# The low halves of the recurrent unit's input weights, made and stored during the first feed-forward

## The chip, the cores and the metric

The kernel runs on one core of a Trainium2 chip. TensorE (PE) multiplies, VectorE (DVE), ScalarE (ACT) and GpSimd (POOL) work on tiles in on-chip memory, SyncE (SP) and POOL issue most DMA transfers. The metric is the device time of one launch in microseconds, lower is better; before the change it is 1498.38 us, the median of three runs (1497.87 to 1498.54).

## What is computed

One step of a two-layer backbone on 640 tokens (512 latent, 128 context) of width 1024, all in fp32. Layer 0 mixes tokens with attention, layer 1 with a gated linear recurrence in both directions, and each is followed by a SwiGLU feed-forward of width 2816. The reference, shortened (in the kernel's names `w_in` is `wi`, `w_gu` is `gu`, `w_down` is `dn`, the recurrence's `w_out` is `wlo`, `w_mod` is `wm`):

```python
def _modulate(x, g, shift, scale):                      # adaLN of an RMS norm
    return _rms_norm(x, g) * (1 + scale[:, None, :]) + shift[:, None, :]

def _swiglu(x, w_gu, w_down):
    gate, up = jnp.split(x @ w_gu, 2, axis=-1)
    return (jax.nn.silu(gate) * up) @ w_down

def _lru_mixer(xm, h0, w_in, conv_w, conv_b, w_a, b_a, w_i, b_i, lam, w_out):
    gate, xr = jnp.split(xm @ w_in, 2, axis=-1)
    xc = _centred_depthwise_conv(xr, conv_w, conv_b)
    a_f, b_f = _rglru_coeffs(xc, w_a[0], b_a[0], w_i[0], b_i[0], lam[0])
    a_b, b_b = _rglru_coeffs(xc, w_a[1], b_a[1], w_i[1], b_i[1], lam[1])
    hs_f, hT_f = _linear_scan(a_f, b_f, h0[:, 0], reverse=False)
    hs_b, hT_b = _linear_scan(a_b, b_b, h0[:, 1], reverse=True)
    y = (hs_f + hs_b) * jax.nn.gelu(gate)
    return y @ w_out, jnp.stack([hT_f, hT_b], axis=1)

for i in range(2):                                      # layer 0 attention, layer 1 recurrence
    sh1, sc1, g1, sh2, sc2, g2 = silu(cond) @ w_mod[i] + b_mod[i]
    x = x + g1 * mixer_i(_modulate(x, norm_g[i, 0], sh1, sc1))
    x = x + g2 * _swiglu(_modulate(x, norm_g[i, 1], sh2, sc2), w_gu[i], w_down[i])
y = _rms_norm(x, final_g)
```

## The kernel before

Activations lie transposed, features on the 128 partitions and tokens along a row, as eight tiles of 128 x 640. A weight matrix is cut into tiles of 1024 x 128 (128x1024 on the chip, 512 KB). PE multiplies in a rounded fp32 form, so every operand is split in two: a high part, the value rounded, and a low part, the value minus the high part. A product is the sum of three matmuls for each of eight steps k: high by high (L239), high weight by low activation (L240), low weight by high activation (L241). These three lines are nearly all of PE's work.

`unit` (L170) makes one split weight tile. SP reads it into `raw`, of which there are three buffers for the whole kernel (L165); the high part `whi` is a cast on ACT (L186) or, in a phase whose only shared PSUM tag is `at`, a second transfer on POOL's queue that casts as it lands (L184); the low part `wlo` is a subtraction on DVE (L188). Where a phase has a second set of weight buffers, the same parts are called `whx` and `wlx`. `ws` and `project` then run the tile over the token chunks and hand each filled PSUM bank to an evacuation on DVE or ACT.

The phases follow one another: `start`, `attn`, `ffn0`, `lru`, `ffn1`. `ffn0` first adds the attention's output projection `wo` to `x` (`project`, DVE L639 for the residual, L623 for the low part of the scaled result, L578 for the sum of squares `ssq`), then forms the norm's statistics (`stats`): PE sums squares over partitions (L592, L595), DVE makes `var` (L597), POOL `rs` (L599), DVE the diagonal `dg` (L601), PE spreads it over partitions (`rr`, L609), ACT copies it to `r` (L633). This is done twice, for the second and the first half of the tokens, and `dg` and `rr` have one buffer each. Since the gate and up products do not need `r` (the norm's factor is applied when they are evacuated, DVE L1007, L1015, L1018), PE can run ahead of the statistics, up to five PSUM banks far (three `mm`, two `mx`). The feed-forward runs in three parts of 8, 7 and 7 hidden tiles (`ci` in `ffn`); each has gate and up products (`ws`), then the down projection (`project`; in the last part `project_closing`, which also forms the norm ahead of the recurrent layer: `nv` L614, high part L615 on ACT, low part L616 on DVE).

Beside this runs a generator, `modulations`: `w_mod` comes in 80 tiles of 512 KB over POOL's queue (L264, `mraw`, two buffers), and DVE forms two products with each (L268, `mprod`, one buffer). A call `fill(n)` takes n steps of it, one tile a step; `FG` and the phase's `quota` say how many. What is due sooner is pulled by `need`.

In `lru` the 16 tiles of `wi` are used through `halves` (L1366): eight for `xr`, which goes on to the convolution and the gates (`gp`, L1407), eight for the GeLU gate. `highs` (L1093) are the first matmuls of the output projection that follows.

The order of the instructions on each engine is not written by hand: a scheduler with a model of times sets it when the kernel is built. `pin` and `issue_after` put one instruction behind another in that order. Each engine then runs its list strictly in order.

Of the kernel before, what the change touches and what calls it, by code (L numbers as in the profile page):

```python
# [9 lines left out]
F32 = mybir.dt.float32  # L10
F32R = mybir.dt.float32r
AF = mybir.ActivationFunctionType
ALU = mybir.AluOpType
AX = mybir.AxisListType

P = 128
D = 1024
# [18 lines left out]
NLT = 10  # L36
C0 = 515
LATPR = (slice(0, 512), slice(C0, LW))
FG = (1, 1, 1)
MODS = ((0, 2), (0, 4), (0, 3), (0, 5), (1, 1), (1, 0), (1, 4), (1, 3), (1, 2), (1, 5))  # L40
NB = 2
KH = KT // 2
# [85 lines left out]
class _Step:  # L128
# [38 lines left out]
        self.read = self.nc.sync.dma_start(t, src).ins  # L167
        return t

    def unit(self, src, slot=None, after=None, nx=3, cast=False, raw=None):  # L170
        nc = self.nc
        _, a, b = src.shape
        raw = self.raw(src) if raw is None else raw
        if slot is None:
            self.nu += 1
            slot = "x" if self.wx and self.nu % 2 == 0 else "m"
        if slot == "x":
            hi, lo = self.wxs([P, a, b], nx)
        else:
            hi = self.t([P, a, b], F32R, "whi", 3)  # L180
            lo = self.t([P, a, b], F32R, "wlo", 3)
        if cast or self.ptags == ["at"]:
            with self.pin(self.cast if after else None):
                nc.gpsimd.dma_start(hi, src)  # L184
        else:
            nc.scalar.copy(hi, raw)  # L186
        with self.pin(after):
            self.low = nc.vector.tensor_tensor(lo, raw, hi.bitcast(F32), ALU.subtract).ins  # L188
        return hi, lo
# [70 lines left out]
    def mod_cols(self, l, j, out):  # L260
        nc = self.nc
        for f in range(KT):
            w = self.t([P, D], F32, "mraw", 2, self.sb)
            nc.gpsimd.dma_start(w, self.i["wm"][l * 6 + j - 2, f])  # L264
            for s in range(2):
                prod = self.t([P, D], F32, "mprod", 1, self.sb)
                with self.tc.issue_after(self.anchor) if self.anchor else nullcontext():
                    nc.vector.scalar_tensor_tensor(prod, w, 1.0, self.csb[:, s], ALU.mult, ALU.mult, accum_out=out[:, s, f:f + 1])  # L268
            yield
        nc.vector.tensor_tensor(out, out, self.col(f"bm{l}{j}").unsqueeze(1).broadcast_to([P, 2, KT]), ALU.add)  # L270
# [15 lines left out]
    def modulations(self):  # L286
        yield from self.mod_gate(0, 2)
        yield from self.mod_ss(0, 3, 1)
        yield from self.mod_gate(0, 5)
        yield from self.mod_ss(1, 0, 0)  # L290
        yield from self.mod_ss(1, 3, 1)
        yield from self.mod_gate(1, 2)
        yield from self.mod_gate(1, 5)

    def fill(self, n):
        for _ in range(min(n, self.quota)):
# [697 lines left out]
    def ffn(self, l, hi, lo, fp, last):  # L994
        nc = self.nc
        f0 = 0
        for ci, n in enumerate((8, 7, 7)):
            hhi = self.big()
            hlo = self.big()
            sg = {}  # L1000

            def eg(j):
                def ev(t0, s, ps):
                    if t0:
                        sg[j] = self.t([P, NTOK], F32, "sg", 2, fp)
                    g = sg[j]
                    nc.vector.tensor_tensor(g[:, s], ps, self.rt[:, s], ALU.mult)  # L1007
                    for c, a, b in _pieces(s.start, s.stop):
                        nc.scalar.activation(g[:, a:b], g[:, a:b], AF.Silu, bias=self.bias[:, c:c + 1])
                return ev  # L1010

            def eu(j):
                def ev(t0, s, ps):
                    u = self.t([P, 320], F32, "up", 2, fp)
                    nc.vector.tensor_tensor(u, ps, self.rt[:, s], ALU.mult)  # L1015
                    for c, a, b in _pieces(s.start, s.stop):
                        g = sg[j][:, a:b]
                        nc.vector.scalar_tensor_tensor(g, u[:, a - t0:b - t0], self.bias[:, c:c + 1], g, ALU.add, ALU.mult)  # L1018
                    self.split(hhi[:, j, s], hlo[:, j, s], sg[j][:, s])
                return ev  # L1020
            for j in range(n):
                f = f0 + j
                self.ws(self.i["gu"][l, f], hi, lo, eg(j), FG[0] * (f > 0), CHB)
                self.ws(self.i["gu"][l, NF + f], hi, lo, eu(j), FG[1] * (f > 0), CHB)
            w = self.i["dn"][l, :, :, f0:f0 + n]
            if ci == 2:
                last(w, hhi, hlo, (l, 5))
            else:
                self.project(w, hhi, hlo, (l, 5), done=lambda f: self.fill(FG[2]))
            f0 += n  # L1030


# [330 lines left out]
        c = CI["ba0"] * KT  # L1363
        nc.vector.tensor_scalar(self.hb, self.cols[:, c:c + 4 * KT], 0.5, None, ALU.mult)

    def halves(self, w, hi, lo, ev, after=None, slot=None):  # L1366
        u = self.unit(w, slot, after, 2)
        return [lambda t0=t0, t1=t1, **kw: ev(t0, self.chunk(u, hi, lo, t0, t1, **kw)) for t0, t1 in CHL]

    def lru_xr(self, f, hi, lo, after=None):  # L1370
        xr = self.xrs[f % 2]
        nat = xr[:, 2:514].rearrange("p (r c) -> p c r", r=ROWS)

        def ev(t0, ps):
            for o, a, b, r in ((nat[:, 56:64], 0, 64, ROWS), (nat[:, 0:40], 64, 384, ROWS),
                               (nat[:, 40:56], 384, 512, ROWS), (xr[:, 517:645], 512, 640, 0)):
                if t0 <= a and b <= t0 + 384:
                    v = ps[:, a - t0:b - t0]
                    self.nc.scalar.copy(o, v.rearrange("p (c r) -> p c r", r=r) if r else v)
        return self.halves(self.i["wi"][KT + f], hi, lo, ev, after)  # L1380

    def turn(self, table, step):
        if table != self.table:
# [126 lines left out]
    def lru_gate(self, f, hi, lo, lp, after=None):  # L1510
# [3 lines left out]
        def ev(t0, ps):  # L1514
# [3 lines left out]
                return  # L1518
            for v, o in ((G, G),) if f == KT - 1 else ((ps, G[:, t0:NTOK]), (G[:, 0:t0], G[:, 0:t0])):
                self.turn(AF.Gelu_apprx_tanh, lambda: nc.scalar.activation(o, v, AF.Gelu_apprx_tanh))  # L1520
        return G, self.halves(self.i["wi"][f], hi, lo, ev, after)

    def new_x(self, st):
        pool = st.enter_context(self.tc.tile_pool(name="x", bufs=1, reuse_waits="tile"))
# [6 lines left out]
    def run(self):  # L1531
# [11 lines left out]
        nc.vector.memset(self.ones, 1.0)  # L1543
        self.st = self.t([P, 2 * KT], F32, "st", 1)
        self.cs = self.t([P, 2 * KT], F32, "cs", 1)
        dram = self.ctx.enter_context(tc.tile_pool(name="dram", bufs=1, space=bass.MemoryType.DRAM))
        mpool, xpool = ExitStack(), ExitStack()
        self.csb = self.t([P, 2, D], F32, "csb", 1, mpool.enter_context(tc.tile_pool(name="mods", bufs=1)))
        self.mask = self.t([P, 64], F32, "mask", 1)
# [11 lines left out]
        V = self.big(F32, PITCH)  # L1561
        V = V.rearrange("p k t -> p (k t)")[:, 0:NT * D].rearrange("p (t d) -> p t d", t=NT)
        O = self.big(F32)
        with self.phase("attn", tp=2, sp=2, op=1, quota=24) as ap:
            self.kz = [self.t([P, 2, 960], F32R, f"KZ{j}", 1, ap) for j in range(2)]

# [29 lines left out]
        self.new_x(xpool)  # L1596
        self.load_x(i["x"])
        xd = dram.tile([D, NTOK], F32, tag="xd", name="xd")
        with self.phase("ffn0", at=2, rr=1, mx=2, wx=2, quota=56) as fp:
            self.project(i["wo"], ohi, olo, (0, 2), ((0, 1), xhi, xlo), None, True)  # L1600

            def last(w, hhi, hlo, gk):
                self.nh, self.nl = self.big(n=PITCH), self.big(n=PITCH)
                self.project_closing(w, hhi, hlo, gk, (1, 0), self.nh, self.nl, xd)
            self.ffn(0, xhi, xlo, fp, last)
        xpool.close()
        mpool.close()
        xhi, xlo = self.nh, self.nl
# [73 lines left out]
```

## Time and profile before

| | before |
|---|---|
| median of three runs | 1498.38 us |
| profiled execution | 1496.74 us |
| its span | 1494.9 us |
| instructions | 26171 |
| ACT busy | 698.6 us (47%) |
| POOL busy | 225.7 us (15%) |
| DMA traffic | 198.88 MB, mean 133 GB/s |

The profile is one execution. Busy times are those of each engine's own instructions; a line such as L188 is a line of the kernel before. `x16` is a count, and in square brackets stands the idle time before an instruction with what ended it. The profiled execution lies 1.64 us below the median of the three runs, and 1.84 us of it lie outside the span.

### The profile page before, as it was taken

The numbers are of one execution on the slowest core, as the hardware profiler recorded it, in microseconds if no ns is written. First come the engines' busy times: TensorE is split into PE (matmuls) and PEld (weight loads), VectorE is DVE, ScalarE is ACT, GpSimd is POOL, SyncE is SP. The second block draws the span as 40 slices with busy tenths as digits, with TensorE's granted clock in tenths as the row PEclk, the third lists the DMA queues.
The fourth block names the chain that finished last, engine by engine and source line by source line (L and its number), as shares of the span: only waits on it lengthen the run. The fifth ranks groups of instructions, "written<-read, shape, count | busy, mean of one in ns | idle before, by whom it ended". The sixth has DMA issues, their size and how long they took to land. (4 is left out here: it accounts for less than half of the span.)

```text
span 1494.9 us, 26171 instructions
## 1 busy us (share of the span) xinstructions
PE 1475.9 (99%) x10399; PEld 1433.0 (96%) x10399; DVE 1062.0 (71%) x2019; ACT 698.6 (47%) x1269; POOL 225.7 (15%) x264
## 2 busy tenths in 40 slices
PE   9999999999999999999999999999999999999997
PEld 7999999899999999999999988899999999999997
DVE  5778998679999987444443769886975666655645
ACT  5676667754332123312321569875634343424243
POOL 0212132101111110000000100000331322232311
PEclk9999999999999999999999999999999999999999
DMA  9645665345566664222222444335333131313111
GB/s 378 201 128 177 196 189 163 105 156 183 196 187 195 207 197 142 63 85 85 66 62 96 142 145 126 115 115 194 102 130 98 57 114 57 113 57 111 59 57 71
DMA packets 73050, 198.88 MB, mean 133 GB/s; under 512 B 8128, under 2 KB 24672, under 8 KB 72800
## 3 DMA queue, kind: packets, MB, share of 16 engines
q1 hardware_dynamic: 57360, 142.31, 29.9%
q0 software_dynamic: 14960, 54.21, 11.8%
q8 instruction: 82, 1.34, 0.4%
q10 hardware_dynamic: 608, 0.69, 0.1%
q14 instruction: 40, 0.33, 0.1%
HBM read 181.05 MB, written 8.92 MB: 127 GB/s over the span
## 5 line engine op out<-in xcount | busy, mean ns | idle before, releaser
L240 PE MATMUL mm<-big,whi 128*128 128x320 f32 (+3 forms) x1193 | 371.2, 311 | 0.8 <-DVE big L1508 0.6
L239 PE MATMUL mm<-big,whi 128*128 128x320 f32 (+3 forms) x1193 | 369.0, 311 | 1.6 <-ACT big L615 0.6
L241 PE MATMUL mm<-big,wlo 128*128 128x320 f32 (+3 forms) x1193 | 368.8, 310 | 0.0
L239 PEld LDWEIGHTS mm<-big,whi 128*128 128x128 f32 x1193 | 223.9, 188 | 3.7 <-ACT big L615 0.9
L240 PEld LDWEIGHTS mm<-big,whi 128*128 128x128 f32 x1193 | 224.2, 188 | 2.8 <-DVE big L1508 1.0
L241 PEld LDWEIGHTS mm<-big,wlo 128*128 128x128 f32 x1193 | 224.7, 188 | 1.1
L268 DVE SCALAR_TENSOR_TENSOR mprod<-mraw,csb 128x1024 f32<-128x1024 f32 x160 | 194.8, 1218 | 11.3 <-DMA mraw<-in_wm 10.8
L639 DVE SCALAR_TENSOR_TENSOR x<-mm,G,x 128x128 f32<-128x128 f32 (+3 forms) x193 | 77.4, 433 | 78.5 <-PE mm L241 77.0
L186 ACT CAST whi<-raw 128x1024 fp32r<-128x1024 f32 (+1 forms) x70 | 72.8, 1040 | 106.1 <-PE mm L240 71.2
L188 DVE TENSOR_TENSOR wlo<-raw,whi 128x1024 fp32r<-128x1024 f32 (+1 forms) x87 | 105.1, 1208 | 23.9 <-ACT whi L186 11.0
L240 PE MATMUL mm<-big,whx 128*128 128x320 f32 (+3 forms) x363 | 112.2, 309 | 0.0
L241 PE MATMUL mm<-big,wlx 128*128 128x320 f32 (+3 forms) x363 | 112.1, 309 | 0.0
L239 PE MATMUL mm<-big,whx 128*128 128x320 f32 (+3 forms) x363 | 111.9, 308 | 0.0
L264 POOL DMA_DIRECT2D mraw<-in_wm x80 | 43.4, 543 | 355.5 <-DVE mprod L268 257.3
L240 PE MATMUL mx<-big,whi 128*128 128x320 f32 (+3 forms) x299 | 92.1, 308 | 0.0
L239 PE MATMUL mx<-big,whi 128*128 128x320 f32 (+3 forms) x299 | 91.9, 307 | 0.0
L241 PE MATMUL mx<-big,wlo 128*128 128x320 f32 (+3 forms) x299 | 91.8, 307 | 0.0
L186 ACT CAST whx<-raw 128x1024 fp32r<-128x1024 f32 (+1 forms) x38 | 39.1, 1028 | 94.1 <-PE mm L240 54.5
L1506 ACT CAST whi<-raw 128x1024 fp32r<-128x1024 f32 (+1 forms) x41 | 41.3, 1007 | 69.0 <-PE mm L240 43.0
L240 PE MATMUL mx<-big,whx 128*128 128x320 f32 (+3 forms) x234 | 72.9, 312 | 0.0
L241 PE MATMUL mx<-big,wlx 128*128 128x320 f32 (+3 forms) x234 | 72.6, 310 | 0.0
L239 PE MATMUL mx<-big,whx 128*128 128x320 f32 (+3 forms) x234 | 72.4, 309 | 0.0
(409 smaller groups left out, 3734.3 us busy)
## 6 DMA issues: line engine op xcount, KB each, us to landing
raw<-in_gu SPq DMA_DIRECT2D x88, 512.0 KB, 3.5
mraw<-in_wm POOLq DMA_DIRECT2D x80, 512.0 KB, 3.9
raw<-in_dn SPq DMA_DIRECT2D x24, 512.0 KB, 3.6
sw<-in_wm SPq DMA_DIRECT2D x16, 512.0 KB, 10.2
raw<-in_wqk SPq DMA_DIRECT2D x16, 512.0 KB, 4.9
raw<-in_wi SPq DMA_DIRECT2D x16, 512.0 KB, 3.5
whi<-in_wi POOLq DMA_DIRECT2D x16, 512.0 KB, 3.8
raw<-in_dn SPq DMA_DIRECT2D x16, 448.0 KB, 3.3
```

The source lines that it names most:

```text
L186: nc.scalar.copy(hi, raw)
L188: self.low = nc.vector.tensor_tensor(lo, raw, hi.bitcast(F32), ALU.subtract).ins
L239: nc.tensor.matmul(ps, hi[:, k], xhi[:, k, s], start=(k == 0), stop=False)
L240: nc.tensor.matmul(ps, hi[:, k], xlo[:, k, s], start=False, stop=False)
L241: self.done = nc.tensor.matmul(ps, lo[:, k], xhi[:, k, s], start=False, stop=(k == last)).ins
L264: nc.gpsimd.dma_start(w, self.i["wm"][l * 6 + j - 2, f])
L268: nc.vector.scalar_tensor_tensor(prod, w, 1.0, self.csb[:, s], ALU.mult, ALU.mult, accum_out=out[:, s, f:f + 1])
L639: self.added = self.nc.vector.scalar_tensor_tensor(xs, ps[:, a - t0:b - t0], G[:, s, f:f + 1], xs, ALU.mult, ALU.add).ins
L1506: self.nc.scalar.copy(hi, v)
```

## The change

After the last modulation the generator goes on with `lows`: for each of the 16 tiles of `wi`, in the order in which the recurrent layer will ask for them, POOL's queue fetches the high part by a casting transfer into an `mprod` buffer (two of them now, in `ffn0`) and the raw tile into an `mraw` buffer; a step later DVE subtracts in place (L313, placed behind the last matmul that was issued so far) and POOL's queue writes the result, 512 KB, to a tile in DRAM (L315). In `lru`, `unit` gets that tile as `low`: SP reads it straight into `wlo` (L189), and the raw read and the subtraction of L188 are not there any more for these 16 tiles, nor are the two pins that held them (`self.sq`, `self.dg`, which go with the subtraction). `FG` now gives the gate and up products of part 1 two steps a call, and the first down projection one step a call and the second two; the quota of `ffn0` goes from 56 to 73 steps (56, 16 tiles, and the step that finishes the last).

```diff
--- before.py
+++ after.py
@@ -36,7 +36,7 @@
 NLT = 10
 C0 = 515
 LATPR = (slice(0, 512), slice(C0, LW))
-FG = (1, 1, 1)
+FG = (1, 2, 1)
 MODS = ((0, 2), (0, 4), (0, 3), (0, 5), (1, 1), (1, 0), (1, 4), (1, 3), (1, 2), (1, 5))
 NB = 2
 KH = KT // 2
@@ -167,10 +167,11 @@
         self.read = self.nc.sync.dma_start(t, src).ins
         return t
 
-    def unit(self, src, slot=None, after=None, nx=3, cast=False, raw=None):
+    def unit(self, src, slot=None, after=None, nx=3, cast=False, raw=None, low=None):
         nc = self.nc
         _, a, b = src.shape
-        raw = self.raw(src) if raw is None else raw
+        if low is None:
+            raw = self.raw(src) if raw is None else raw
         if slot is None:
             self.nu += 1
             slot = "x" if self.wx and self.nu % 2 == 0 else "m"
@@ -184,6 +185,9 @@
                 nc.gpsimd.dma_start(hi, src)
         else:
             nc.scalar.copy(hi, raw)
+        if low is not None:
+            nc.sync.dma_start(lo.bitcast(F32), low)
+            return hi, lo
         with self.pin(after):
             self.low = nc.vector.tensor_tensor(lo, raw, hi.bitcast(F32), ALU.subtract).ins
         return hi, lo
@@ -263,7 +267,7 @@
             w = self.t([P, D], F32, "mraw", 2, self.sb)
             nc.gpsimd.dma_start(w, self.i["wm"][l * 6 + j - 2, f])
             for s in range(2):
-                prod = self.t([P, D], F32, "mprod", 1, self.sb)
+                prod = self.t([P, D], F32, "mprod", self.mb, self.sb)
                 with self.tc.issue_after(self.anchor) if self.anchor else nullcontext():
                     nc.vector.scalar_tensor_tensor(prod, w, 1.0, self.csb[:, s], ALU.mult, ALU.mult, accum_out=out[:, s, f:f + 1])
             yield
@@ -291,6 +295,26 @@
         yield from self.mod_ss(1, 3, 1)
         yield from self.mod_gate(1, 2)
         yield from self.mod_gate(1, 5)
+        yield from self.lows()
+
+    def lows(self):
+        nc = self.nc
+        held = None
+        for key, src in self.split_ahead + [(None, None)]:
+            if key is not None:
+                shape = list(src.shape)
+                raw = self.t(shape, F32R, "mraw", 2, self.sb)
+                hi = self.t(shape, F32R, "mprod", 2, self.sb)
+                nc.gpsimd.dma_start(hi, src)
+                nc.gpsimd.dma_start(raw.bitcast(F32), src)
+            if held:
+                k, r, h = held
+                with self.pin(self.done):
+                    nc.vector.tensor_tensor(r, r.bitcast(F32), h.bitcast(F32), ALU.subtract)
+                self.low_parts[k] = self.dram.tile(list(r.shape), F32, tag=f"low{k[0]}{k[1]}", name=f"low{k[0]}{k[1]}")
+                nc.gpsimd.dma_start(self.low_parts[k], r.bitcast(F32))
+            held = key and (key, raw, hi)
+            yield
 
     def fill(self, n):
         for _ in range(min(n, self.quota)):
@@ -1020,13 +1044,13 @@
                 return ev
             for j in range(n):
                 f = f0 + j
-                self.ws(self.i["gu"][l, f], hi, lo, eg(j), FG[0] * (f > 0), CHB)
-                self.ws(self.i["gu"][l, NF + f], hi, lo, eu(j), FG[1] * (f > 0), CHB)
+                self.ws(self.i["gu"][l, f], hi, lo, eg(j), FG[ci == 1] * (f > 0), CHB)
+                self.ws(self.i["gu"][l, NF + f], hi, lo, eu(j), FG[ci == 1] * (f > 0), CHB)
             w = self.i["dn"][l, :, :, f0:f0 + n]
             if ci == 2:
                 last(w, hhi, hlo, (l, 5))
             else:
-                self.project(w, hhi, hlo, (l, 5), done=lambda f: self.fill(FG[2]))
+                self.project(w, hhi, hlo, (l, 5), done=lambda f: self.fill(FG[f0 > 0]))
             f0 += n
 
 
@@ -1363,8 +1387,8 @@
         c = CI["ba0"] * KT
         nc.vector.tensor_scalar(self.hb, self.cols[:, c:c + 4 * KT], 0.5, None, ALU.mult)
 
-    def halves(self, w, hi, lo, ev, after=None, slot=None):
-        u = self.unit(w, slot, after, 2)
+    def halves(self, k, hi, lo, ev, after=None):
+        u = self.unit(self.i["wi"][k], None, after, 2, low=self.low_parts["i", k])
         return [lambda t0=t0, t1=t1, **kw: ev(t0, self.chunk(u, hi, lo, t0, t1, **kw)) for t0, t1 in CHL]
 
     def lru_xr(self, f, hi, lo, after=None):
@@ -1377,7 +1401,7 @@
                 if t0 <= a and b <= t0 + 384:
                     v = ps[:, a - t0:b - t0]
                     self.nc.scalar.copy(o, v.rearrange("p (c r) -> p c r", r=r) if r else v)
-        return self.halves(self.i["wi"][KT + f], hi, lo, ev, after)
+        return self.halves(KT + f, hi, lo, ev, after)
 
     def turn(self, table, step):
         if table != self.table:
@@ -1518,7 +1542,7 @@
                 return
             for v, o in ((G, G),) if f == KT - 1 else ((ps, G[:, t0:NTOK]), (G[:, 0:t0], G[:, 0:t0])):
                 self.turn(AF.Gelu_apprx_tanh, lambda: nc.scalar.activation(o, v, AF.Gelu_apprx_tanh))
-        return G, self.halves(self.i["wi"][f], hi, lo, ev, after)
+        return G, self.halves(f, hi, lo, ev, after)
 
     def new_x(self, st):
         pool = st.enter_context(self.tc.tile_pool(name="x", bufs=1, reuse_waits="tile"))
@@ -1543,7 +1567,10 @@
         nc.vector.memset(self.ones, 1.0)
         self.st = self.t([P, 2 * KT], F32, "st", 1)
         self.cs = self.t([P, 2 * KT], F32, "cs", 1)
-        dram = self.ctx.enter_context(tc.tile_pool(name="dram", bufs=1, space=bass.MemoryType.DRAM))
+        self.dram = dram = self.ctx.enter_context(tc.tile_pool(name="dram", bufs=1, space=bass.MemoryType.DRAM))
+        self.low_parts = {}
+        order = [KT, 0, KT + 1] + [k for f in range(1, KT) for k in ((f, KT + f + 1) if f + 1 < KT else (f,))]
+        self.split_ahead = [(("i", k), i["wi"][k]) for k in order]
         mpool, xpool = ExitStack(), ExitStack()
         self.csb = self.t([P, 2, D], F32, "csb", 1, mpool.enter_context(tc.tile_pool(name="mods", bufs=1)))
         self.mask = self.t([P, 64], F32, "mask", 1)
@@ -1561,6 +1588,7 @@
         V = self.big(F32, PITCH)
         V = V.rearrange("p k t -> p (k t)")[:, 0:NT * D].rearrange("p (t d) -> p t d", t=NT)
         O = self.big(F32)
+        self.mb = 1
         with self.phase("attn", tp=2, sp=2, op=1, quota=24) as ap:
             self.kz = [self.t([P, 2, 960], F32R, f"KZ{j}", 1, ap) for j in range(2)]
 
@@ -1596,13 +1624,15 @@
         self.new_x(xpool)
         self.load_x(i["x"])
         xd = dram.tile([D, NTOK], F32, tag="xd", name="xd")
-        with self.phase("ffn0", at=2, rr=1, mx=2, wx=2, quota=56) as fp:
+        self.mb = 2
+        with self.phase("ffn0", at=2, rr=1, mx=2, wx=2, quota=73) as fp:
             self.project(i["wo"], ohi, olo, (0, 2), ((0, 1), xhi, xlo), None, True)
 
             def last(w, hhi, hlo, gk):
                 self.nh, self.nl = self.big(n=PITCH), self.big(n=PITCH)
                 self.project_closing(w, hhi, hlo, gk, (1, 0), self.nh, self.nl, xd)
             self.ffn(0, xhi, xlo, fp, last)
+            assert next(self.mods, None) is None
         xpool.close()
         mpool.close()
         xhi, xlo = self.nh, self.nl
```

With other calls of `fill` and other work on DVE, the scheduler also puts old instructions in another order. In the kernel after, lines between `unit` and `modulations` stand 4 lower (L188 is L192, L268 is L272), those from `fill` on 24 lower or a little more (L601 is L625). Three places follow; the names are those of the tiles, output before input.

DVE in the opening of `ffn0`, from the statistics' first `var` on; before:

```order
L597 TENSOR_SCALAR var_4713<-at_4706 128x3
L597 TENSOR_SCALAR var_4731<-at_4724 128x3
L268 SCALAR_TENSOR_TENSOR mprod_5322,G_680_3223<-mraw_5320,csb_83 128x1024
L268 SCALAR_TENSOR_TENSOR mprod_5324,G_680_3223<-mraw_5320,csb_83 128x1024
L601 TENSOR_TENSOR dg_4717<-ident_65,rs_4715 128x384
L188 TENSOR_TENSOR wlx_5172<-raw_5169,whx_5171 128x1024
L270 TENSOR_TENSOR G_680_3223<-G_680_3223,cols_61 128x16
L268 SCALAR_TENSOR_TENSOR mprod_5394,A_1023_5391<-mraw_5392,csb_83 128x1024
L268 SCALAR_TENSOR_TENSOR mprod_5396,A_1023_5391<-mraw_5392,csb_83 128x1024
L601 TENSOR_TENSOR dg_4735<-ident_65,rs_4733 128x384
L268 SCALAR_TENSOR_TENSOR mprod_5469,A_1023_5391<-mraw_5467,csb_83 128x1024
L1007 TENSOR_TENSOR sg_4779<-mx_4752,r_4705 128x320
```

DVE at the same place after the change:

```order
L621 TENSOR_SCALAR var_4713<-at_4706 128x3
L272 SCALAR_TENSOR_TENSOR mprod_5539,A_1023_5391<-mraw_5537,csb_83 128x1024
L272 SCALAR_TENSOR_TENSOR mprod_5541,A_1023_5391<-mraw_5537,csb_83 128x1024
L621 TENSOR_SCALAR var_4731<-at_4724 128x3
L625 TENSOR_TENSOR dg_4717<-ident_65,rs_4715 128x384
L192 TENSOR_TENSOR wlx_5172<-raw_5169,whx_5171 128x1024
L272 SCALAR_TENSOR_TENSOR mprod_5614,A_1023_5391<-mraw_5612,csb_83 128x1024
L272 SCALAR_TENSOR_TENSOR mprod_5616,A_1023_5391<-mraw_5612,csb_83 128x1024
L192 TENSOR_TENSOR wlo_5242<-raw_5239,whi_5241 128x1024
L625 TENSOR_TENSOR dg_4735<-ident_65,rs_4733 128x384
L1031 TENSOR_TENSOR sg_4779<-mx_4752,r_4705 128x320
```

In both, the first evacuation that frees a PSUM bank is the row with `sg<-mx` and `r` (the last row, L1007 and L1031). The second `dg` (`dg_4735`) is the ninth row behind the first `var` in both; before, four products and one subtraction stand between, now four products and two subtractions, and two of the products have come ahead of the second `var` and of the first `dg`. The products themselves are later ones (`mprod_5469` stands ahead of the first `var`, where before `mprod_5249` did): six more have been put ahead of the statistics.

PE in the opening of `ffn0`, around the `rr` matmuls; before, the second of the two:

```order
L241 MATMUL mm_4891<-big_4125,wlx_4882 128x322
L239 MATMUL mm_4891<-big_4125,whx_4881 128x322
L240 MATMUL mm_4891<-big_4126,whx_4881 128x322
L609 MATMUL rr_4737<-dg_4735,ones_74 128x128 x3
L241 MATMUL mm_4891<-big_4125,wlx_4882 128x322
L239 MATMUL mm_4891<-big_4125,whx_4881 128x322
L240 MATMUL mm_4891<-big_4126,whx_4881 128x322
```

PE after the change, both of them:

```order
L243 MATMUL mm_4891<-big_4125,whx_4881 128x322
L244 MATMUL mm_4891<-big_4126,whx_4881 128x322
L245 MATMUL mm_4891<-big_4125,wlx_4882 128x322
L633 MATMUL rr_4719<-dg_4717,ones_74 128x128 x3
L633 MATMUL rr_4737<-dg_4735,ones_74 128x128 x3
L243 MATMUL mx_4922<-big_4125,whx_4881 128x320
L244 MATMUL mx_4922<-big_4126,whx_4881 128x320
```

Before, 25 matmuls stand between the two groups `rr`, and 13 more behind the second before a bank is used that must have been evacuated. Now the two stand together, 21 matmuls behind the statistics (before, 43 to the first), and the next row, `mx_4922`, starts a bank that DVE has to free. Ahead of the statistics stand 60 matmuls more than before.

DVE at the end of `ffn0`, where the norm ahead of the recurrent layer is formed; before:

```order
L188 TENSOR_TENSOR wlo_9560<-raw_9557,whi_9559 128x1024
L616 SCALAR_TENSOR_TENSOR big_8920<-nv_9382,B_1108_6023,big_8919 128x384
L616 SCALAR_TENSOR_TENSOR big_8920<-nv_9386,B_1108_6023,big_8919 128x384
L614 SCALAR_TENSOR_TENSOR nv_9445<-x_4130,A_1023_5391,rr_9250 128x384
L597 TENSOR_SCALAR var_9462<-at_9453 128x2
L614 SCALAR_TENSOR_TENSOR nv_9449<-x_4130,A_1023_5391,rr_9250 128x384
L616 SCALAR_TENSOR_TENSOR big_8920<-nv_9445,B_1108_6023,big_8919 128x384
L601 TENSOR_TENSOR dg_9466<-ident_65,rs_9464 128x256
L188 TENSOR_TENSOR wlo_9566<-raw_9563,whi_9565 128x1024
```

DVE after the change, from the corresponding low part on:

```order
L640 SCALAR_TENSOR_TENSOR big_9032<-nv_9498,B_1108_6023,big_9031 128x384
L602 TENSOR_TENSOR ssq_9062<-ssq_9062,sq_9526 128x256
L638 SCALAR_TENSOR_TENSOR nv_9557<-x_4130,A_1023_5391,rr_9362 128x384
L638 SCALAR_TENSOR_TENSOR nv_9561<-x_4130,A_1023_5391,rr_9362 128x384
L621 TENSOR_SCALAR var_9574<-at_9565 128x2
L640 SCALAR_TENSOR_TENSOR big_9032<-nv_9557,B_1108_6023,big_9031 128x384
L640 SCALAR_TENSOR_TENSOR big_9032<-nv_9561,B_1108_6023,big_9031 128x384
L625 TENSOR_TENSOR dg_9578<-ident_65,rs_9576 128x256
```

The subtractions `wlo_9560` and `wlo_9566` (L188), and one some seventeen rows further up, are gone; the norm's rows close up.

## Prediction

> **What bounds the kernel now.** I read the busy times first, then the busy times by stretch, then PE's waits.
>
> ```profile
> span 1494.9 us, 26171 instructions
> PE 1475.9 (99%) x10399; PEld 1433.0 (96%) x10399; DVE 1062.0 (71%) x2019; ACT 698.6 (47%) x1269; POOL 225.7 (15%) x264
> ...
> PEclk9999999999999999999999999999999999999999
> ```
>
> PE is busy all but 19.0 us of the span, so work that goes from another engine is worth at most the PE idle time that it ends, and work that comes costs only where it makes PE idle. Where that can be, the stretches show (length, busy time of PE, of its weight loads, DVE, ACT, POOL, then clock, DMA share, GB/s):
>
> ```profile
> core 0: us, PE busy (x) PEld busy (x) DVE busy (x) ACT busy (x) POOL busy (x), PEclk, DMA share, GB/s
> 325.00:375.00 50.00, 50.00 (x349) 50.00 (x348) 46.86 (x93) 22.42 (x44) 5.76 (x9) 1.00 0.56 175
> ...
> 525.00:575.00 50.00, 50.00 (x342) 50.00 (x341) 44.98 (x81) 13.47 (x26) 5.92 (x11) 1.00 0.63 198
> 575.00:625.00 50.00, 50.00 (x341) 50.00 (x340) 25.77 (x48) 16.12 (x33) 0.55 (x1) 1.00 0.30 87
> 625.00:675.00 50.00, 50.00 (x344) 50.00 (x343) 20.51 (x35) 9.53 (x12) 0.00 (x0) 1.00 0.26 79
> ...
> 825.00:850.00 25.00, 23.57 (x161) 22.27 (x159) 23.46 (x63) 11.76 (x30) 2.03 (x9) 1.00 0.46 149
> 850.00:875.00 25.00, 24.47 (x159) 21.73 (x159) 12.27 (x14) 14.19 (x25) 2.16 (x4) 1.00 0.59 180
> 875.00:1000.00 125.00, 124.94 (x766) 112.04 (x765) 110.56 (x131) 107.42 (x141) 6.87 (x13) 1.00 0.39 117
> 1000.00:1025.00 25.00, 23.50 (x162) 23.23 (x161) 19.18 (x37) 8.25 (x15) 0.56 (x1) 1.00 0.75 273
> ```
>
> In `ffn0` (from 325 to 825 us) PE does not idle, though DVE is busy 46.86 of 50 us as long as modulations run, and about half or less behind 575. In and around the recurrent layer PE idles 1.43 + 0.53 + 0.06 + 1.50 = 3.52 us. That is all that this layer can give; the other 15.5 us of idle time lie ahead of `ffn0` or in and behind the last feed-forward, where PE's order stays as it was.
>
> **The recurrent layer: what goes away.** The subtractions, and the waits there:
>
> ```profile
> L188 DVE TENSOR_TENSOR wlo<-raw,whi 128x1024 fp32r<-128x1024 f32 x16 | 19.6, 1224 | 11.5 <-DMA whi<-in_wi 5.0 <-issue 4.6 <-PE gp L1407 1.9
> ```
>
> This row holds 13 tiles of `wi` and three of the next projection; three more of `wi` stand ahead of it, so 16 x 1.22 = 19.6 us of DVE go. Between 875 and 1000 us PE idles 0.06 us although DVE is busy 110.56 of 125, so there they lie beside PE and are worth 0, as are the 16 raw reads, which the 16 reads of `low` replace. What remains is the edge:
>
> ```profile
> 827.00 1.22 DVE L188 TENSOR_TENSOR wlo<-raw,whi 128x1024 fp32r<-128x1024 f32 x1 [1.45 <-DMA whi<-in_wi]
> ...
> 835.97 1.21 DVE L188 TENSOR_TENSOR wlo<-raw,whi 128x1024 fp32r<-128x1024 f32 x1
> ...
> 840.32 1.22 DVE L188 TENSOR_TENSOR wlo<-raw,whi 128x1024 fp32r<-128x1024 f32 x1
> ```
>
> ```profile
> 836.11 0.49 PE L592 MATMUL at<-ones,ssq 128*128 128x128 f32 x2 [0.66 <-DVE ssq L578]
> ...
> 839.47 0.44 PE L239 MATMUL mm<-big,whi 128*128 128x384 f32 x1 [0.56 <-ACT big L615]
> 840.12 0.44 PE L240 MATMUL mm<-big,whi 128*128 128x384 f32 x1 [0.21 <-DVE big L616]
> 850.64 0.39 PE L239 MATMUL mm<-big,whi 128*128 128x256 f32 x1 [0.53 <-ACT xr L1379]
> ```
>
> DVE is at its limit here (23.46 of 25). Two subtractions and the 1.45 us in which it stood waiting for a transfer precede 839.47: 1.2 + 1.45 + 1.2 = 3.9 us earlier for the norm's rows, more than the 0.56 + 0.21 that PE waits for them. The third, at 840.32, holds the rows from which the next chunk's `xr` comes, 0.53. The 0.66 is the statistics' own chain from the last residual, and stays. **Gain 1.3 us**; bounds 0 (the `wlo` reads on SP's queue come late, in its order behind the stores of `x`) and 1.97 (all four). I take 1.3, since a read needs what these did:
>
> ```profile
> mraw<-in_wm POOLq DMA_DIRECT2D x80, 512.0 KB, 3.9
> ...
> raw<-in_wi SPq DMA_DIRECT2D x16, 512.0 KB, 3.5
> whi<-in_wi POOLq DMA_DIRECT2D x16, 512.0 KB, 3.8
> ...
> out_nv<-big SPq DMA_DIRECT2D x1, 512.0 KB, 4.5
> ```
>
> A `low` lands like its `whi`, 3.5 beside 3.8 us, once PE frees the buffer, and the subtraction behind both is saved. At the layer's other end:
>
> ```profile
> 1002.00 0.41 PE L1093 MATMUL mm<-big,whi 128*128 128x320 f32 x1 [1.50 <-ACT big L1481]
> ```
>
> ```profile
> L186 ACT CAST whi<-raw 128x1024 fp32r<-128x1024 f32 (+1 forms) x70 | 72.8, 1040 | 106.1 <-PE mm L240 71.2
> ```
>
> This wait is the tail of the last tile's gates through ACT and DVE. In the new order PE has 12 matmuls more between the last gates and this row (12 x 0.15 = 1.8 us of cover), but a cast of the output weights (1.04) has moved into ACT's chain: 1.8 - 1.0 = **0.8 us gained**; bounds 0 and 1.5.
>
> **The opening of `ffn0`: a new wait.** Here the change costs, by its order alone. First PE and DVE before:
>
> ```profile
> 366.62 0.61 PE L592 MATMUL at<-ones,ssq 128*128 128x128 f32 x4
> ...
> 369.22 0.39 PE L240 MATMUL mx<-big,whx 128*128 128x322 f32 x1
> ...
> 375.67 0.83 PE L609 MATMUL rr<-dg,ones 128*128 128x128 f32 x6
> ...
> 376.63 0.31 PE L239 MATMUL mx<-big,whi 128*128 128x320 f32 x1
> ...
> 378.10 0.31 PE L240 MATMUL mx<-big,whi 128*128 128x320 f32 x1
> ...
> 380.03 0.83 PE L609 MATMUL rr<-dg,ones 128*128 128x128 f32 x6
> ```
>
> ```profile
> 369.28 0.38 DVE L597 TENSOR_SCALAR var<-at 128x3 f32<-128x3 f32 x2 [2.70 <-PE at L595]
> 369.59 1.22 DVE L268 SCALAR_TENSOR_TENSOR mprod<-mraw,csb 128x1024 f32<-128x1024 f32 x1
> ...
> 372.00 0.55 DVE L601 TENSOR_TENSOR dg<-ident,rs 128x384 f32<-128x384 f32 x1
> 372.48 1.22 DVE L188 TENSOR_TENSOR wlx<-raw,whx 128x1024 fp32r<-128x1024 f32 x1
> ...
> 376.60 0.56 DVE L601 TENSOR_TENSOR dg<-ident,rs 128x384 f32<-128x384 f32 x1 [0.41 <-PE rr L609]
> ...
> 378.22 0.49 DVE L1007 TENSOR_TENSOR sg<-mx,r 128x320 f32<-128x320 f32 x1
> ```
>
> ```profile
> 369.52 2.00 POOL L599 TENSOR_TENSOR rs<-var,mhalf 128x3 f32<-128x3 f32 x2 [2.12 <-DVE var L597]
> ```
>
> Call S the start of the statistics' matmuls (366.62). They take 2.6 us; the second `dg` is done at 376.60 + 0.56, S + 10.5; PE asks for it at 380.03, S + 13.4, because 68 matmuls stand between (one each 0.147 us: ten steps from 376.63 to 378.10). So the chain is hidden, with 2.9 us to spare.
>
> After: 60 matmuls (8.8 us) have moved ahead of the statistics, where they cover six more products on DVE (6 x 1.22 = 7.3 us; DVE idled 2.70 there, so S comes without a wait). Behind S only 21 are left. DVE, by the order in the section on the change: first `var` S + 1.8 (seven of the twelve rows of statistics, and a wake-up), done 2.0; two products (1.2 from start to start) to 4.4; second `var` and first `dg` (its `rs`, 1.0 on POOL, is done at 3.1) to 5.1; `wlx` 6.2; two products 8.6; `wlo` 9.75; second `dg` 10.25. PE: 2.6 + 21 x 0.147 = 5.7; first `rr` to 6.3; then it stands before the second until about 10.3. **Cost 4.0 us.** Queued behind that `rr` is everything that PE has; the row behind it needs a bank that DVE frees with the first L1031, 0.45 us after the `dg`, while `rr` itself takes 0.6, so nothing is added. Bounds: 3 (second `dg` a product earlier than reckoned) to 6 (a product waits 2 us for its transfer: 3.9 us of landing, two buffers). Nothing later pays it back, since PE has no other gap until 836.
>
> **The lows themselves.** 16 subtractions x 1.22 = 19.5 us on DVE between about 570 and 670, where 54 of 100 us are free, and 48 transfers of 512 KB, 25 MB in 100 us, 250 GB/s on top of 79 to 87. Hidden, **cost 0**, as long as a pair of tiles (two buffers) turns fast enough: store 0.5 + 4.5, raw reads 2 x 0.5 + 3.9, subtraction 1.2, 11.1 us for what the order spaces by 13.6 us of matmuls on average (7 to 17.6). Behind a subtraction that waits, DVE's evacuations wait, and PE has 4 to 13 us of banks in hand. Bounds 0 to 20 (below). Freeing DVE earlier from modulations gains nothing, as PE idles nowhere there.
>
> **Sum.** 4.0 - 1.3 - 0.8 + 0 = +1.9 us on the profiled execution: 1496.74 + 1.9 = 1498.6. That execution lies 1.64 below the median, so as a median **1500.3 us**, +0.13%.
>
> **Rivals.**
> - *The lows are late* (0.17; the slower side). Place: 570 to 670 us. If landings stretch by half (6.75 and 5.85), a pair takes 14.3 us or more against 13.6, and the closer-set pairs, at 7, run over what the banks hold: 8 pairs x 0.7 = 5.6 plus those, about +6, so 1506; doubled landings 19.5 us a pair, 8 x 5.9 less up to 13, +34. It decides from some 13.6 us a pair. Against it: 4.5 and 3.9 come from stretches that were loaded too (0.63 DMA share, 198 GB/s beside products). For it: no row has stores at 330 GB/s in all, nor POOL's queue with 48 transfers in order. [...]
> - *No wait in the opening* (0.13). Only if DVE's chain is shorter than I reckon, or PE's 99 matmuls later. Then -1.3 - 0.8 = -2.1, 1496.3; with every gap of the layer closed -3.5, 1494.9, just faster by what can be told. It is also the limit of the reading that the layer gains from 19.6 us less on DVE: the change does that, and PE does not care.
> - *The layer gains nothing* (0.15): late `low` reads on SP. Then +4.0, 1502.4.
> - *PE's clock drops after the gap* (0.05). The granted clock is 1.00 in every row above, but no gap there exceeds 1.5 us. Were it halved for as long as the gap, 4.0 us would do 2.0 us of work: +2.0, 1502.3. [...]
>
> **Chances.** The forecast itself has 0.5. A measurement here tells about 0.2% (3.0 us) from no change: below 1495.4 or above 1501.4. Faster: half of the second rival and a little of the forecast, 0.08. Slower: the first, most of the third and fourth, and the forecast's upper part (stall near 6), 0.36. Within: 0.56. The range runs from all gaps closed without a new wait (1495.0) to the lows late by half (1506): 1495 to 1506.5.
>
> **What would show it.** Right: a PE wait of about 4 us at the second `rr` (L633) on DVE `dg` (L625) near 382 to 386 us, with DVE busy throughout; no PE wait on `big` L615/L616's successors near 840; the wait at L1093's successor at half or less; L188's successor gone from the layer; PE gapless from 390 to 830. Wrong: PE waits on DVE between 570 and 680 (first rival), on a `wlo` read near 835 (third), or a granted clock under 1.00 behind 386 (fourth); or less than 2 us idle at the second `rr`.

## The result and the profile after

After the change the kernel takes 1507.29 us (median of four runs, 1507.05 to 1514.11) against 1498.12 us before: 1.0074 of it, 95% interval 1.006 to 1.0089. It is 9 us slower where +1.9 was forecast, and lies just outside the range. The profiled execution took 1507.14 us.

The head of the page after, with busy times as before:

```profile
span 1505.4 us, 26235 instructions
PE 1479.3 (98%) x10399; PEld 1436.5 (95%) x10399; DVE 1059.2 (70%) x2019; ACT 699.3 (46%) x1269; POOL 257.0 (17%) x312
```

The span grew by 10.5 us. PE idles 26.1 us in place of 19.0, and the same 10399 matmuls keep it busy 3.4 us longer. So about 7 us are waits, and about 3.4 us matmuls that ran slower. PE's waits (sum, times, longest):

```profile
PE mm L244 <- DVE big L1532: 7.3, 3, 6.5
PE rr L633 <- DVE dg L625: 3.3, 1, 3.3
...
PE mm L1117 <- ACT big L1505: 0.8, 1, 0.8
...
PE mm L243 <- ACT xr L1403: 0.3, 1, 0.3
```

The wait at the second `rr` is the one forecast; 6.5 us for a low part of a hidden tile (L1532, L1508 before) is new; the two in and behind the recurrent layer are what is left of 1.50 and 0.53. Stretches before the change are shown with the prediction, but for this one, around the opening of `ffn0` (length, PE, weight loads, DVE, ACT, POOL, clock, DMA share, GB/s):

```profile
375.00:400.00 25.00, 25.00 (x174) 25.00 (x173) 24.09 (x45) 10.52 (x21) 3.23 (x6) 1.00 0.59 198
```

After the change:

```profile
375.00:400.00 25.00, 21.66 (x146) 21.50 (x145) 22.31 (x41) 10.07 (x19) 6.11 (x7) 0.93 0.56 175
625.00:650.00 25.00, 20.81 (x142) 20.55 (x140) 13.05 (x22) 5.79 (x12) 5.38 (x10) 0.99 0.85 291
650.00:675.00 25.00, 22.74 (x142) 22.74 (x143) 12.23 (x18) 4.00 (x4) 5.37 (x10) 0.87 0.80 276
825.00:850.00 25.00, 25.00 (x198) 25.00 (x197) 15.13 (x36) 7.50 (x16) 2.53 (x4) 1.00 0.46 142
850.00:875.00 25.00, 24.73 (x163) 23.44 (x163) 15.15 (x42) 14.84 (x34) 2.85 (x10) 1.00 0.52 180
1000.00:1025.00 25.00, 24.22 (x168) 23.96 (x168) 21.98 (x37) 12.80 (x19) 2.68 (x5) 1.00 0.55 190
```

Three things are to be seen. The recurrent layer's start lost nearly all its idle time (1.96 to 0.27 us), its end half (1.50 to 0.78): 2.4 us gained. At the two new waits (the first three rows) the granted clock is below 1.00, which before the change it was in no stretch ahead of 1475 us. And between 625 and 675 the DMA engines are busy at 0.80 to 0.85.

Closer, around the wait at `rr` and the one near 650:

```profile
386.00:388.00 2.00, 2.00 (x13) 2.00 (x14) 2.00 (x6) 1.75 (x5) 0.00 (x0) 0.72 0.72 279
388.00:390.00 2.00, 2.00 (x9) 2.00 (x9) 2.00 (x7) 0.24 (x2) 0.50 (x1) 0.50 0.56 215
390.00:392.00 2.00, 2.00 (x15) 2.00 (x14) 2.00 (x5) 1.08 (x3) 0.04 (x1) 0.93 0.52 127
...
652.00:654.00 2.00, 1.74 (x6) 1.74 (x7) 2.00 (x5) 0.94 (x1) 1.41 (x3) 0.50 0.42 174
654.00:656.00 2.00, 2.00 (x9) 2.00 (x9) 1.40 (x2) 0.00 (x0) 1.27 (x3) 0.50 0.92 119
656.00:658.00 2.00, 2.00 (x14) 2.00 (x13) 0.55 (x1) 0.00 (x0) 0.00 (x0) 0.87 0.95 303
```

PE is busy, but at clock 0.50 nine matmuls start in 2 us in place of some fifteen. Busy time hides this loss; the clock column and the counts show it.

The wait near 650, on DVE, and then on POOL's queue (start, duration, and in brackets the idle time before it and what ended it):

```profile
642.57 1.08 DVE L192 TENSOR_TENSOR wlo<-raw,whi 128x896 fp32r<-128x896 f32 x1
650.58 1.23 DVE L313 TENSOR_TENSOR mraw<-mraw,mprod 128x1024 fp32r<-128x1024 f32 x1 [6.93 <-DMA mraw<-in_wi]
651.72 0.48 DVE L1532 TENSOR_TENSOR big<-sg,big 128x320 fp32r<-128x320 f32 x1
```

```profile
638.42 0.54 POOL L315 DMA_DIRECT2D lowi<-mraw  x1 [1.00 <-DVE mraw L313]
638.95 0.54 POOL L308 DMA_DIRECT2D mprod<-in_wi  x1
639.51 0.54 POOL L309 DMA_DIRECT2D mraw<-in_wi  x1
643.80 0.54 POOL L309 DMA_DIRECT2D mraw<-in_wi  x1 [3.75 <-DMA lowi<-mraw]
652.10 0.54 POOL L315 DMA_DIRECT2D lowi<-mraw  x1 [7.76 <-DVE mraw L313]
```

DVE stands 6.93 us before a low's subtraction, until its raw tile lands; the low part of a hidden tile that PE needs (L1532) is the next row of its list. PE is then in the down projection of the second part, which needs that part's last hidden tile, and so cannot run further ahead. The raw reads of that pair were issued at 639.51 and 643.80, the later one only when a store had landed and freed the buffer. DVE's wait is for the first of the two, which landed 10.9 us after its issue (view of the tile `mraw`, 639.2 to 640.2 us). How long transfers took there (from the DMA view of 560 to 690 us: count, KB, median us to landing):

```profile
mraw<-in_wi POOLq DMA_DIRECT2D x16, 512.0 KB, 7.5
mprod<-in_wi POOLq DMA_DIRECT2D x16, 512.0 KB, 6.5
lowi<-mraw POOLq DMA_DIRECT2D x16, 512.0 KB, 4.0
```

### The profile page after: what moved, and what is told of

It is laid out like the page before. It is cut to its first block, busy times and chain, and to the rows that moved or that the text cites. A ratio compares the mean times of both kernels' runs of the same rounds, so it can differ in the third digit from the quotient of the medians.

```text
span 1505.4 us, 26235 instructions
## 1 busy us (share of the span) xinstructions
PE 1479.3 (98%) x10399; PEld 1436.5 (95%) x10399; DVE 1059.2 (70%) x2019; ACT 699.3 (46%) x1269; POOL 257.0 (17%) x312
## 5 line engine op out<-in xcount | busy, mean ns | idle before, releaser
L272 DVE SCALAR_TENSOR_TENSOR mprod<-mraw,csb 128x1024 f32<-128x1024 f32 x160 | 193.4, 1227 | 3.5 <-DMA mraw<-in_wm 3.2
L268 POOL DMA_DIRECT2D mraw<-in_wm x80 | 43.6, 545 | 334.1 <-DVE mprod L272 253.5
L192 DVE TENSOR_TENSOR wlo<-raw,whi 128x1024 fp32r<-128x1024 f32 (+1 forms) x71 | 85.7, 1206 | 10.0 <-ACT whi L187 9.8
L244 PEld LDWEIGHTS mm<-big,whx 128*128 128x128 f32 x363 | 68.4, 188 | 6.7 <-DVE big L1532 6.7
L244 PE MATMUL mx<-big,whx 128*128 128x320 f32 (+3 forms) x234 | 73.6, 315 | 0.0
L1530 ACT CAST whi<-raw 128x1024 fp32r<-128x1024 f32 (+1 forms) x41 | 41.4, 1010 | 68.5 <-PE mm L244 43.7
```

The source lines that it names most:

```text
L244: nc.tensor.matmul(ps, hi[:, k], xlo[:, k, s], start=False, stop=False)
L1530: self.nc.scalar.copy(hi, v)
```

## The experiments

All times are medians, ratios are to the kernel before on the same chip, where it took 1497.57 us (for `lru_only`, `twobuf`, `onebuf` and `spread`) and 1497.61 us (for the other four). The excerpts of code show the lines that matter; `...` marks what is left out.

**The layer's half alone (`lru_only`).** `low0` is a stand-in, one stored tile for all 16.

```diff
@@ the kernel before, with unit(low=...) as in the change
+            if ahead and f == 2:
+                self.low0 = self.dram.tile([P, KT, P], F32, tag="low0", name="low0")
+                nc.gpsimd.dma_start(self.low0, u[0].bitcast(F32))
...
-        u = self.unit(w, slot, after, 2)
+        u = self.unit(w, slot, after, 2, low=self.low0)
```

> The kernel before, with the recurrent layer's half of the change alone: the 16 low parts are read from DRAM as after the change, but from one stand-in tile that is stored once early in ffn0 (a high part of the output projection's weights), so the layer's values are not the reference's; no lows are made. Theory: the layer itself gained about 2.5 us after the change (PE waits 1.7 us shorter at its start, 0.7 at its end), so 1498.1 - 2.5 = 1495.6 us, PE idle at 825 to 875 us falling from 1.96 to 0.3 us. Rival: the gain is only shifted time from the stalls ahead of it, then 1498.1 and the waits at the layer's start as before.

1494.28 us, 0.9977 (0.9968 to 0.9986), 3.3 us faster. PE idles 0.27 us from 825 to 875, as after the change. The theory holds, with a gain somewhat above the 2.5 us read from the waits; the spans of the two profiled executions, 1494.9 and 1492.6, differ by 2.3 us.

**A second product buffer alone (`twobuf`).**

```diff
@@ the kernel before
-                prod = self.t([P, D], F32, "mprod", 1, self.sb)
+                prod = self.t([P, D], F32, "mprod", self.mb, self.sb)
...
+        self.mb = 1
         with self.phase("attn", tp=2, sp=2, op=1, quota=24) as ap:
...
+        self.mb = 2
         with self.phase("ffn0", at=2, rr=1, mx=2, wx=2, quota=56) as fp:
```

> The kernel before with one edit, two mprod buffers in ffn0; no lows, FG and the quota as before. Theory: the second product buffer alone makes the scheduler put the products ahead of the statistics, so the 3.3 us wait at the second rr and the clock of one half behind it (about 1.7 us) come with it: 1498.1 + 5.0 = 1503.1 us. Rival: the wait comes from the new FG and quota (more steps to place), then 1498.1 and no wait at rr.

1503.36 us, 1.0039 (1.0025 to 1.0053). Of its waits and stretches:

```profile
PE rr L609 <- DVE dg L601: 3.3, 1, 3.3
```

```profile
384.00:386.00 2.00, 0.00 (x0) 0.00 (x0) 2.00 (x4) 0.83 (x1) 0.59 (x1) 0.94 0.83 274
386.00:388.00 2.00, 1.60 (x7) 1.63 (x8) 2.00 (x5) 1.20 (x4) 0.00 (x0) 0.50 0.75 238
388.00:390.00 2.00, 2.00 (x10) 2.00 (x9) 2.00 (x6) 0.60 (x3) 0.00 (x0) 0.50 0.68 254
390.00:392.00 2.00, 2.00 (x9) 2.00 (x9) 1.13 (x4) 0.96 (x2) 0.54 (x1) 0.50 0.36 113
392.00:394.00 2.00, 2.00 (x14) 2.00 (x13) 1.63 (x3) 0.46 (x1) 0.00 (x0) 0.85 0.55 215
```

The same wait, and a longer stretch at half clock: 5.8 us lost with not one low in the program. The rows of DVE and PE in the opening are those after the change. That the second buffer alone makes the scheduler put more products ahead is shown; by which of its rules was not tried.

**One product buffer again (`onebuf`).**

```diff
@@ the kernel after, lows()
-                hi = self.t(shape, F32R, "mprod", 2, self.sb)
+                hi = self.t(shape, F32R, ("mprod", "mhi")[n % 2], 1, self.sb)
...
-        self.mb = 2
```

> The kernel after with one edit: products keep one mprod buffer, and the lows' high parts alternate between that buffer and one of their own, so the lows still have two. Theory: the opening of ffn0 is as before (no wait at rr), and the wait of 6.5 us with its clock drop near 650 stays: 1507.3 - 5.0 = 1502.3 us. Rival (the opening wait comes from FG): 1507.3.

1501.14 us, 1.0022 (1.0013 to 1.0032), with runs from 1498.36 to 1503.79. No wait at `rr`, clock 1.00 there. The late wait is still there, 6.1 us in the profiled execution:

```profile
PE mm L243 <- ACT big L1530: 6.5, 2, 6.1
```

Here the part that PE needs is the hidden tile's high part, made on ACT (L1530), which waits for a row of DVE behind the low (`sg`, L1042).

**PE kept at work in the wait (`twobuf_warm`).**

```diff
@@ twobuf, the method spread(), ahead of the second rr
+        if "rr" in self.ptags and t0 == 0:
+            a = self.rr
+            for _ in range(10):
+                with self.pin(a):
+                    a = nc.tensor.matmul(ps[:, 0:P], self.ones, self.ident, start=True, stop=True).ins
```

> As twobuf (3.3 us wait at the second rr, 1503.4 us), with ten 128x128 matmuls of constants put on PE between the two rr groups, into the bank that the second rr overwrites: about 10 x 0.22 = 2.2 us of work inside the wait, nothing else. Theory (the granted clock falls to one half because PE stands still for over 3 us): the clock stays at 1.00 from 384 to 394 us, and the time falls by what the slow matmuls cost, about 3 us, to 1500.4 us. Rival (the lower clock is chance, or belongs to the power of that stretch): 1503.4 us and the clock at 0.50 near 388 as in twobuf.

1501.48 us, 1.0023 (1.0013 to 1.0033): 1.9 us less than `twobuf` although 40 more PE instructions run. The clock stays:

```profile
386.00:388.00 2.00, 2.00 (x16) 2.00 (x16) 2.00 (x5) 1.60 (x5) 0.00 (x0) 1.00 0.91 315
388.00:390.00 2.00, 2.00 (x16) 2.00 (x15) 2.00 (x6) 0.14 (x1) 0.54 (x1) 1.00 0.33 127
```

So it was the standing still that lowered the clock here: PE idled 3.33 us from 382 to 388 us in `twobuf`, and 0.74 us in this run. The medians put the lower clock's own loss at 1.9 us, less than the 3 expected; the spans of the two profiled executions, 1502.0 and 1498.9, put it at 3.1.

**Fewer transfers (`chip_hi`).**

```diff
@@ onebuf, lows()
-                nc.gpsimd.dma_start(hi, src)
                 nc.gpsimd.dma_start(raw.bitcast(F32), src)
+                nc.scalar.copy(hi, raw.bitcast(F32))
```

> As onebuf, but the lows' high part is a cast on ACT of the raw tile, in place of a second casting read: 32 transfers of 512 KB in place of 48, the loop through buffers and DRAM stores as it was. Theory (the 48 transfers fill the DMA engines, which stretches landings to 7 us and a pair of tiles to 14.7 us): raw reads land in about 4.5 us, a pair takes under 13 us, DVE waits less than 3 us for any low, no wait of PE near 640: 1498.1 - 2.5 = 1495 us. Rival (the loop store, raw read, subtraction is too long as such, whatever the traffic): waits of 5 to 8 us on DVE and the PE wait stay, 1501 us.

1505.93 us, 1.0056 (1.0041 to 1.0071), worse than `onebuf`: my theory as stated falls. Its PE waits, the landings from 560 to 720 us, and the first of its two groups of subtractions (first and last start):

```profile
PE mm L243 <- ACT big L1530: 12.7, 2, 12.3
```

```profile
mraw<-in_wi POOLq DMA_DIRECT2D x16, 512.0 KB, 4.3
lowi<-mraw POOLq DMA_DIRECT2D x16, 512.0 KB, 5.1
```

```profile
L313 DVE TENSOR_TENSOR mraw<-mraw,mprod x8: 1216/1224/1226, 581.6 to 672.3; 128x1024 fp32r<-128x1024 f32 x8
```

Raw reads land in 4.3 us, as expected, at a DMA share of 0.58 from 560 to 720 us. But a pair still takes (672.3 - 581.6) / 7 = 13.0 us. The cast on ACT is a new step of the loop, some 1.05 us each. And in POOL's list a read that waits for one buffer's store stands ahead of the other buffer's store, so only one store is under way at a time; which of the two makes the 13.0 was not tried. DVE's order, besides, now sets the lows closer: counted in PSUM banks evacuated between the first and the last low (24 matmuls of 0.147 us for each, 21 in the down projection), 81 us of PE's work, where `onebuf` has 94 and the kernel after 96. On the chip the same stretch took 96, 103 and 109 us: 15, 9 and 13 more, and PE waited 12.3, 6.1 and 6.5 us. So here the wait came not from full DMA engines as such, but from a loop that was longer than the spacing in which the scheduler, with its own idea of the loop, wove the lows into DVE's list.

**The subtractions on POOL (`pool_sub`).**

```diff
@@ onebuf, lows()
-                with self.pin(self.done):
-                    nc.vector.tensor_tensor(r, r.bitcast(F32), h.bitcast(F32), ALU.subtract)
+                nc.gpsimd.tensor_tensor(r, r.bitcast(F32), h.bitcast(F32), ALU.subtract)
```

> As onebuf, but the 16 subtractions of the lows run on POOL, so nothing of DVE waits for a low; transfers as in onebuf. Theory (PE waits because evacuations stand in DVE's queue behind a subtraction that waits for its transfer): no wait of PE in ffn0 although raw reads still land in 6 to 8 us: about 1495 us. Rival (the full DMA engines delay the weights themselves): PE still waits in ffn0, 1500 us or more.

1494.54 us, 0.9979 (0.997 to 0.9988). PE does not wait in `ffn0`, although the weights' own reads are slowed there (3.5 us before):

```profile
raw<-in_gu SPq DMA_DIRECT2D x16, 512.0 KB, 6.0
```

The raw reads landed in 4.7 us, not the 6 to 8 that I named, and not for a lighter load: from 560 to 720 us the DMA share is 0.76, in `onebuf` about 0.72 (an estimate from the slices of its DMA view of 560 to 820 us). In POOL's list a subtraction (2.4 us) now stands between a tile's high part and its raw read, and behind the raw read come a store and the next tile's high part; it is the high parts that land late:

```profile
mraw<-in_wi POOLq DMA_DIRECT2D x16, 512.0 KB, 4.7
mprod<-in_wi POOLq DMA_DIRECT2D x8, 512.0 KB, 7.1
mhi<-in_wi POOLq DMA_DIRECT2D x7, 512.0 KB, 7.3
```

The wait for the raw tiles has not gone: POOL itself stands 43.9 us in all before the subtractions, where DVE stood 36.2 in `onebuf`. A subtraction takes 2.4 us on POOL against 1.2 on DVE, and PE waits for none of it. So what cost time was the waiting at the head of DVE's list, and not the slower reads of the weights.

**The lows spread (`spread`), and without their pins (`spread_unpinned`).** `spread` also takes the lows out of the modulations' generator and, in the second down projection, sets some of them behind the sum into `x`; `spread_unpinned` lacks only the last line of the code below.

```diff
@@ onebuf, ffn() of layer 0, and lows()
+                if ci == 2 or ci == 1 and j > 1:
+                    self.step(self.evac)
...
-                with self.pin(self.done):
+                with self.pin(self.behind):
```

> As onebuf, but the 16 lows are spread: each subtraction is queued on DVE behind the evacuation of a hidden tile, one per 12 to 14 us of PE's time from about 565 to 795 us, in place of one per 6.8; the modulations' steps are called earlier (FG 2). Theory (the wait near 650 comes from DMA engines filled by 48 transfers in 110 us, so that a low waits at the head of DVE's queue): no wait in ffn0, the layer's gain of 2.5 us stays, 1495.6 us, and raw reads land in 4 to 5 us in place of 7.5. Rival (16 more subtractions on DVE delay evacuations as such, wherever they stand): waits of PE on DVE remain in ffn0 and the time is 1498 or more.

1493.98 us, 0.9978 (0.9968 to 0.9987): 3.6 us faster than before the change. The lows run from 592 to 784 us, raw reads land in 4.6 us, and PE does not wait in `ffn0`:

```profile
560.00:660.00 100.00, 100.00 (x682) 100.00 (x681) 62.32 (x107) 28.01 (x54) 13.39 (x25) 1.00 0.65 210
660.00:760.00 100.00, 100.00 (x682) 100.00 (x681) 51.63 (x81) 27.69 (x52) 12.41 (x24) 1.00 0.58 191
```

> As spread, but the subtractions are pinned as in the change, behind a matmul. Theory (a pin orders one engine's list only, so a pin on a PE instruction holds nothing on DVE, and the scheduler takes the lows as soon as its model has them ready): the lows come bunched again though the calls are spread, a PE wait of some us comes back, 1498 to 1502 us. Rival (the spread calls alone do it): 1494 us like spread.

1501.39 us, 1.0021 (1.0011 to 1.0031), from 1496.85 to 1503.18, with a PE wait of 4.9 us as in `onebuf`:

```profile
PE mm L243 <- ACT big L1535: 5.3, 2, 4.9
```

It differs from `spread` in the pin alone, and DVE's rows from 560 to 700 us are those of `onebuf`, one by one, though the calls are spread. So a pin orders only the list of the engine of the instruction that it names. `self.done` is a matmul, and the pin in the change holds nothing on DVE; the section on the change says that L313 stands behind the last matmul, and this is not so.

## Why the prediction was wrong

- **What bounds the kernel: right.** PE bounds it, and 19.6 us less on DVE in the layer is worth only the edges: 1.3 + 0.8 = 2.1 us forecast, 1.7 + 0.7 = 2.4 read from the waits, 3.3 measured alone (`lru_only`). Part by part it was less good: the 0.66 us that was to stay went too, and 0.27 of the 0.53 that was to go stayed.
- **The wait in the opening: right in place and cause, 3.3 us for 4.0.** The second `dg` was done at S + 9.8 for 10.25, and the first `rr` ended at S + 6.6 for 6.3. `twobuf` adds what was not known: the second product buffer makes it, not `FG`.
- **The clock: a rival at 0.05 and +2.0 us, and it came**, once behind each wait. PE is busy 3.4 us longer over both. Before the change it is under 1.00 only behind PE's last matmul (0.50 from 1490 to 1495 us); that a gap between matmuls would halve it, and for as long as the gap, no row then showed: it was the prediction's assumption. Afterwards it was 0.50 for 3.4 us behind the opening's gap of 3.33 us, but for 6.8 in `twobuf` behind one of the same length, where 6.2 us of PE's work at half clock cost about 3.1. So the rival's size was right for one gap; its chance was wrong, since it rested on gaps of 1.5 us at most, where the gap that the sum itself forecast was 4.0.
- **The lows at cost 0: this step failed.** The sum took a pair of tiles at 11.1 us against a spacing of 13.6. The loop took 108.6 / 7.5 = 14.5 us (16 lows have 15 intervals, 7.5 pairs), because raw reads land in 7.5 us, not 3.9; stores took 4.0 for 4.5. The spacing was 96 / 7.5 = 12.8 when counted from the first to the last low. And it was taken as an average to be compared with, while the shortfall adds up over the pairs: 13 us by the last, of which PE waited 6.5, the slow clock behind that wait took about 2 (4.3 us of work at 0.50, an estimate from the rows above), and the banks in hand covered the rest. So in place of 0 stand 6.5 us of waiting in one go and the clock behind it, some 8.5 us together. This is the rival "the lows are late", which got 0.17, and its place is right. That its +6 comes near the 6.5 is luck: with reads and stores half longer the same terms add up to 15.3 us a pair, not 14.3, and so to 8 x 1.7 = 13.6 us before the banks; the reads nearly doubled, the stores did not stretch at all; and the clock was left out. I had taken the landings from rows with less traffic: 198 GB/s at a DMA share of 0.63, where the lows ran at 288 GB/s and 0.84 (567 to 676 us). Landings of 7.5 against 3.9 us on POOL's queue and of 6.1 against 3.5 for SP's reads of `gu` came with that traffic, but are not shown to come from it alone: in `pool_sub` the raw reads land in 4.7 us at a DMA share of 0.76, in `onebuf` in 7.1 at about 0.72 (both 560 to 720 us), so their place in POOL's own list counted too. `chip_hi` shows a loop that takes 13 us even with reads at 4.3.

By terms, on the profiled executions: 3.3 + 6.5 of waits, 3.4 of slow clock, less 2.4, is 10.8 us; the span grew by 10.5. Removing the opening's wait (`onebuf`) and then the lows' (`spread`, `pool_sub`) leaves the layer's gain alone, 3.6 and 3.1 us beside 3.3. What stays open is why the time of the late wait varies so between executions (`onebuf` 1498.4 to 1503.8, and one run of the kernel after at 1514.11).

## What to carry to other kernels

Work for an idle engine is not free when it waits at the head of a list that a busy engine depends on (here PE waited 6.5 us in one go; in `pool_sub` and `spread` it did not): put it on an engine that nobody waits for, or pin it behind an instruction of its own engine, at a spacing longer than its measured loop. Compare a loop with its spacing pair by pair, since the shortfall adds up, and reckon the loop with landings under the traffic that the change itself makes, in the order in which its queue issues them (raw reads: 3.9 us before, 7.5 after the change, 4.7 in `pool_sub`). A buffer added for one use changes the order of every other use of that tag (`twobuf`: 5.8 us).

## What the runs showed of the hardware

A PE gap of 3.3 us was followed by a clock of 0.50, for 3.4 us after the change and 6.8 us in `twobuf` (worked out from the clock column of the 2 us rows); with ten 128x128 matmuls inside the gap (`twobuf_warm`) the clock stayed at 1.00. The gap of 1.50 us before the change (1002 us) left it at 1.00. A read of 512 KB that landed in 3.9 us at a DMA share of 0.61 (before, 325 to 575 us) took 7.5 us at 0.80 to 0.85 (after, 575 to 675 us), where POOL issues it behind the high part's read; where a subtraction on POOL stands between the two and the next high part's read is issued behind it (`pool_sub`, share 0.76 from 560 to 720 us), it took 4.7 us, and the high part's read 7.1 to 7.3. POOL subtracted 128x1024 in 2.4 us (`pool_sub`) where DVE took 1.2 (`onebuf`), and PE did not wait for it.
